# Places outside the ring for the first gate, up and input tiles, and differential heads first in the output projection

## The chip, the core and the metric

The kernel runs on one core of a Trainium2 chip. The core has a matrix engine (TensorE, PE in the profile, with its weight loads as PEld), a vector engine (VectorE, DVE), a scalar engine (ScalarE, ACT), GpSimd (POOL) and SyncE (SP). Each runs its own list of instructions in order; they wait for one another through semaphores. Data comes from HBM by DMA, which SP and POOL issue here. The metric is the device time of one execution in microseconds. Three runs of the kernel before took 2190.43 to 2191.55 us, with a median of 2191.18 us.

## The reference

Two layers of a hybrid trunk over 256 tokens of width 2048, in float32:

```python
for l in range(DEPTH):                       # 2 layers
    h = rms_norm(x, pre_mix_norm[l])
    m = hybrid_mixer(h, l, w_in[l], w_o[l], ...)
    x = x + rms_norm(m, post_mix_norm[l])
    h = rms_norm(x, pre_ffn_norm[l])
    f = swiglu(h, w_gate[l], w_up[l], w_down[l])
    x = x + rms_norm(f, post_ffn_norm[l])
```

The mixer projects h with `w_in` (2048 x 6144) into the parts of 8 stick-breaking heads and 8 differential heads, runs both kinds of attention with a norm for each head, concatenates the heads (stick-breaking ones first) and projects them with `w_o` (2048 x 2048). `swiglu` is `(silu(h @ w_gate) * (h @ w_up)) @ w_down` with an inner width of 5632.

## The kernel before

**Weights.** Almost all time goes into the products of 256 tokens with the weight matrices, and all weights pass through once. They are cut into pieces of 256 rows (a pair kp of 128-row blocks) by 512 columns (a column tile c), 512 KB each, and lie in DRAM in the order in which they are used; `weight_order` writes this order down and `plan` holds the number of each piece. A piece i goes through three steps:

- `fetch(upto)` (L201 to L228) lets SP load pieces up to number `upto`, into a ring of four "raw" buffers. A load waits until the buffer is free, that is until the lo of the piece four earlier in the ring is done.
- `feed(upto)` (L275 to L293) splits each into two parts of reduced precision, hi (a copy by ScalarE, L286) and lo = raw - hi (VectorE, L289). Both go into rings of six buffers, tags "hi" and "lo".
- `weights(i, ahead)` (L312) feeds up to `LOOKAHEAD` = 4 pieces beyond the one that is used next, and hands out the parts.

A product is then three matmuls: hi with the hi of the activations, lo with hi, and hi with lo (L536 to L538 in the output projection, L1036 to L1038 elsewhere).

**Sevens.** For some pairs kp, the gate and up pieces (or two column tiles of another matrix) are taken together as the right side of a 2 x 2 block product that needs seven products instead of eight (`seven_products`). These need sums of the two pieces. In the feed-forward part SP loads one piece into a tile G (L209) and the other into a tile T (L237), and a second DMA, issued by POOL, adds the first half of G's piece into T (L238). From G and T `mixed_weights` (L241 ff.) makes hi and lo of both, then T = T - T and G = G + T on VectorE (L267, L268), and of these Th (ScalarE, L259) and Tl (VectorE, L260). `EARLY` and `LEAD` say how far ahead of its use T is loaded. The scheduler of the framework decides in which place of SP's queue T and G come among the raws.

**Output projection.** Sixteen units first do the column tiles c = 0 and 1 (order `KP_O`), then c = 2 and 3 run over `LATE_O`, of which the pairs 5 and 6 (`O_SEVEN`) are formed as a seven. Pairs 0 to 3 are the stick-breaking heads (tiles mix_sb), 4 to 7 the differential heads (mix_df). The last two pairs, `LAST_O`, are left for an ending that is written out by hand for ScalarE and VectorE (L1131 ff.): the four units (c, kp) of token tile t = 0, each column tile then evacuated, squared and weighted (`evac_sum`, L556 to L559), `rescale` (L565 to L570 and L443 f., and L582, which adds the result to x), and then the four units of t = 1, with one group of transposes of the new x (L452, 128x128 each) behind each unit. xF, the normed and transposed x in hi and lo, comes from the transposes through ScalarE (L455) and VectorE (L460). In between stand the calls that feed and fetch the pieces that come next; their numbers are counted from `idx`, the first of the last four units: `idx` to `idx + 3` belong to the output projection, `idx + 4` and `idx + 5` are the first gate and up pieces, and so on.

**Gate and up.** Eleven column tiles of 512 follow. The first runs its pairs in the order (0, 1, 3, 2, 7, 4, 6, 5), of which 4 and 6 are sevens; its pairs 0 and 1 are done for t = 0 first and then for t = 1. The products of t = 1 begin while the transposes of t = 1 are still to come. The second column tile has sevens at 4, 5 and 6. Then come the down projection and, between the layers, the input projection of the second layer, whose activations xI come from transposes of xd (also L452), fed by `rescale` (L582).

**Rooms.** The pool `rooms` holds places of 128 x 1024 floats, four of tag "early" and four of tag "late". The early ones hold x at the start, later the mixed outputs of the differential heads, then the first four activation tiles; the late ones hold pieces and halves of x at other times. An early room of the differential heads comes free when the last unit that reads them is done.

Of the kernel before, what the change touches and what calls it, by code (L numbers as in the profile page):

```python
# [10 lines left out]
F32R = mybir.dt.float32r  # L11
# [6 lines left out]
P = 128  # L18
D = 2048
S = 256  # L20
L = 2
# [4 lines left out]
CW = 512  # L26
# [5 lines left out]
URGENT = 50  # L32
TAIL = 3
KP_O = (4, 5, 6, 7, 0, 1, 2, 3)
LATE_O = (4, 5, 0, 1, 6, 2)
LAST_O = (3, 7)
O_SEVEN = (5, 6)
PAIRS = ((6, 8), (10, 7), (9, 0), (11, 2), (1, 3), (4, 5))
IN_SEVEN = (4, 5)
# [5 lines left out]
FIRST_ORDER = (0, 1, 3, 2, 7, 4, 6, 5)  # L45
# [21 lines left out]
def weight_order():  # L67

    order = []

    def queue_pair(name, l, kp, c):
        order.append((name, l, kp, c))
        return len(order) - 1

    plan = []
    sevens, plain, own = set(), set(), set()
    for l in range(L):
        lay = {"in": {}, "o": {}, "gate": {}, "up": {}, "down": {}}
        for n, (ca, cb) in enumerate(PAIRS):
            for kp in IN_ORDER if n else range(KT // 2):  # L80
                lay["in"][ca, kp] = queue_pair("w_in", l, kp, ca)
                lay["in"][cb, kp] = queue_pair("w_in", l, kp, cb)
                if kp in IN_NOW[n]:
                    plain.add(lay["in"][cb, kp])
        order_o = [(c, kp) for kp in KP_O for c in (0, 1)]
        order_o += [(c, kp) for kp in LATE_O for c in (2, 3)] + [(c, kp) for c in (2, 3) for kp in LAST_O]
        lay["order_o"] = order_o
        for c, kp in order_o:
            lay["o"][c, kp] = queue_pair("w_o", l, kp, c)
            if c == 3 and kp in O_SEVEN:  # L90
                own.add(lay["o"][c, kp])
        for c in range(FF // CW):
            for kp in FIRST_ORDER if c == 0 else range(KT // 2):
                lay["gate"][c, kp] = queue_pair("w_gate", l, kp, c)
                lay["up"][c, kp] = queue_pair("w_up", l, kp, c)
                if kp in gate_sevens(c):
                    sevens.add(lay["up"][c, kp])
        for half in range(2):
            for kp in range(FF // P // 2):
                for c in (2 * half, 2 * half + 1):  # L100
                    lay["down"][c, kp] = queue_pair("w_down", l, kp, c)
                if kp in DOWN_SEVEN[half]:
                    sevens.add(lay["down"][2 * half + 1, kp])
        plan.append(lay)
    return order, plan, sevens, plain, own
# [48 lines left out]
def kernel(  # L154
# [18 lines left out]
    wpool = ctx.enter_context(tc.tile_pool(name="wpool", bufs=1))  # L173
# [16 lines left out]
    order, plan, sevens, plain, own = weight_order()  # L190
# [6 lines left out]
    def fetch(upto):  # L197
        while len(raws) < min(upto, len(stream)):
            i = len(raws)
            for j in range(i, min(i + EARLY + 1, mix_raw[3])):  # L200
                if j in sevens and j not in sums:  # L201
                    summed(j)
            if i in sevens:
                raws.append(sums[i])
                continue
            if i + 1 in sevens:
                g = mix_raw[0].tile([P, 2, CW], F32, tag="G", bufs=mix_raw[1], name=f"G{i}")
                with not_ahead(i):
                    loads.append(nc.sync.dma_start(g, stream[i]))  # L209
                raws.append(g)  # L210
                continue
            if i in own or i + 1 in own:
                raw = mix_pool[0].tile([P, 2, CW], F32, tag="v", bufs=2, name=f"V{i}")
            elif i in plain or i + 1 in plain:
                raw = late_room([P, 2, CW], f"GU{i}")
            else:
                raw = wpool.tile([P, 2, CW], F32, tag="raw", bufs=4, name=f"raw{i}")
            mixing = bool({i, i + 1} & (own | plain))
            with not_ahead(i) if mixing else nullcontext():
                loads.append(nc.sync.dma_start(raw, stream[i]))  # L220
            raws.append(raw)
            if not mixing:
                usual.append((i, loads[-1]))
# [3 lines left out]
    def not_ahead(i):  # L227

        return tc.issue_after(next(load.ins for j, load in reversed(usual) if j <= i - LEAD))
# [3 lines left out]
    def summed(i):  # L233

        sums[i] = mix_raw[0].tile([P, 2, CW], F32, tag="T", bufs=mix_raw[2], name=f"T{i}")
        with not_ahead(i):
            loads.append(nc.sync.dma_start(sums[i], stream[i]))  # L237
        nc.gpsimd.dma_start(sums[i][:, 0, :], stream[i - 1][:, 0, :], accum_op=ALU.add)  # L238
# [37 lines left out]
    def feed(upto):  # L276
        fetch(upto)
        while fed[0] < min(upto, len(stream)):
            i = fed[0]
            raw = raws[i]  # L280
            if i in sevens or i in plain or i in own:
                ready[i] = mixed_weights(i)
                fed[0] += 1
                continue
            hi = wpool.tile([P, 2, CW], F32R, tag="hi", bufs=6, name=f"hi{i}")
            nc.scalar.activation(hi, raw, AF.Copy)  # L286
            lo = wpool.tile([P, 2, CW], F32R, tag="lo", bufs=6, name=f"lo{i}")
            with behind():
                rest = nc.vector.tensor_tensor(out=lo, in0=raw, in1=hi.bitcast(F32), op=ALU.subtract)  # L289
            ready[i] = (hi, lo)  # L290
            fed[0] += 1
            rests.append(rest)
# [4 lines left out]
    def behind():  # L297

        if held[1] == 0:
            return nullcontext()  # L300
        held[1] -= 1
        return tc.issue_after(held[0].ins)
# [5 lines left out]
    def in_turn():  # L308

        return tc.issue_after(loads[-1].ins)  # L310

    def weights(i, ahead):  # L312
        feed(i + 1 + ahead)
        return ready[i]

    def exp_ln_tables():
# [29 lines left out]
    def late_room(shape, name, dtype=F32):  # L346

        return rooms.tile(shape, dtype, tag="late", name=name)

    def early_room(shape, name, dtype=F32):  # L350

        return rooms.tile(shape, dtype, tag="early", name=name)

    x_pool = [None]

# [237 lines left out]
    def norm_pair(pool, ob, mix, mixed, h0, gcol, nm):  # L593
# [16 lines left out]
        if nm[0] == "d":  # L610
            both = early_room([P, 2, 2, S], f"mix_{nm}", F32R)
# [403 lines left out]
    def seven_in(banks, extra, sums, xT, l, cc, kp, first, last):  # L1015
        hi, lo = weights(plan[l]["in"][cc[0], kp], LOOKAHEAD)
        m = weights(plan[l]["in"][cc[1], kp], LOOKAHEAD)
        seven_products(banks, extra, sums, *pair_blocks(xT, kp), hi, lo, m, first, last)
# [60 lines left out]
    def shared_sign(t, col):  # L1079
        return ALU.subtract if (t, col) == (1, 0) else ALU.add  # L1080

    xT = None
    for l in range(L):
# [27 lines left out]
        open_sums[0] = True  # L1111
        for kp in LATE_O:
            i, j = (plan[l]["o"][c, kp] for c in (2, 3))
            if kp not in O_SEVEN:
                for c, i in ((2, i), (3, j)):
                    unit({t: accs[c, t] for t in range(NT)}, mix, i, kp, range(NT), kp == LATE_O[0], False)
                continue
            if kp == O_SEVEN[0]:
                extra = four_banks(False, [f"{q}_o{l}" for q in ("p1", "p6", "p7", "q5")])
            hi, lo = weights(i, LOOKAHEAD)  # L1120
            m = weights(j, LOOKAHEAD)
            seven_products(got, extra, forms[kp], *pair_blocks(mix, kp), hi, lo, m, kp == O_SEVEN[0], kp == O_SEVEN[-1])
            if kp == O_SEVEN[-1]:
# [3 lines left out]
                for c in (2, 3):  # L1127
                    nc.vector.tensor_tensor(out=accs[c, 1], in0=accs[c, 1], in1=mg[1, 1][:, c - 2, :], op=shared_sign(1, c - 2))
        idx = plan[l]["o"][2, LAST_O[0]]
        last_o = [(c, kp) for c in (2, 3) for kp in LAST_O]  # L1130
        with tc.manual_schedule(engines={mybir.EngineType.Activation, mybir.EngineType.DVE}):  # L1131
            feed(idx + 6)
            for n, (c, kp) in enumerate(last_o):
                unit({0: accs[c, 0]}, mix, idx + n, kp, (0,), False, kp == LAST_O[-1], 0)
                if kp == LAST_O[-1]:
                    evac_sum(pool, accs[c, 0], mg, ssm, gpost, c, 0, f"o{l}")
            rescale(mg, ssm, 0, f"o{l}")
            for n, (c, kp) in enumerate(last_o):
                feed(idx + 7 + n)
                fetch(min(idx + 12 + n, idx + 12))  # L1140
                unit({1: accs[c, 1]}, mix, idx + n, kp, (1,), False, kp == LAST_O[-1], 0)
                transposed(0, 32 + l * KT, xT, cols=(n,))
                if (c, kp) == (2, LAST_O[-1]):
                    evac_sum(pool, accs[2, 1], mg, ssm, gpost, 2, 1, f"o{l}", True)
# [99 lines left out]
        for half in range(2):  # L1244
# [74 lines left out]
            for t in range(NT):  # L1319
# [4 lines left out]
                for c in cc:  # L1324
                    for kp in range(nkp - tail, nkp):
# [3 lines left out]
                        hi, lo = weights(plan[l]["down"][c, kp], LOOKAHEAD)  # L1329
# [66 lines left out]
```

## Time and profile before

| What | Value |
|---|---|
| median of 3 runs | 2191.18 us (2190.43 to 2191.55) |
| profiled execution | 2191.05 us |
| its span in the trace | 2189.4 us |
| granted clock of TensorE | 0.999 |
| data moved | 467.28 MB, mean 213 GB/s |
| raw loads (SP) | 522 of 512 KB, median 4.6 us from issue to landing |
| G loads (SP) | 110 of 512 KB, median 5.8 us |

A profile page gives for each engine its busy time and its number of instructions. A timeline row gives start, length, engine, line, operation, "written <- read" tiles with their shapes, how many equal instructions it joins (x4), and in brackets how long the engine had stood idle before and whose work ended that. A row of the waits view gives an engine and line, what it waited for, the sum, the number of times and the longest. A windows row gives for a stretch of time the busy time of each engine with its count of instructions, the granted clock and the DMA share. Recorded matmuls overlap, so their starts and not their lengths give the pace. Where instructions follow back to back on VectorE, the next one starts some 0.08 us before the recorded end of the last.

### The profile page before, as it was taken

What the parts mean: (1) busy time and instruction counts of PE and PEld (TensorE: products, weight loads), DVE (VectorE), ACT (ScalarE), POOL (GpSimd) and SP (SyncE); (2) the same over time, 40 slices, a digit from 0 to 9 for tenths busy, and PEclk for the clock granted to TensorE, in tenths of its full rate; (3) what the DMA queues carried; (4) which work ended last, traced back from release to release, by engine and by line L of the source; (5) the groups of instructions that cost most, each with busy time, mean ns of one, the idle gap of its engine ahead of it and who ended that gap; (6) DMA issues with size and microseconds to landing.
All of it is one profiled execution on the core that took longest, in us unless ns stands there. A gap on an engine that the chain in (4) does not pass through costs nothing.

```text
span 2189.4 us, 28540 instructions
## 1 busy us (share of the span) xinstructions
PE 2174.9 (99%) x9988; PEld 1791.1 (82%) x9988; DVE 1901.3 (87%) x2610; ACT 1370.9 (63%) x2051; POOL 139.1 (6%) x187
## 2 busy tenths in 40 slices
PE   9999999999999999999999999999999999999998
PEld 7888888888888888888878888888888888888886
DVE  6888658999999999989878886589999999999997
ACT  7666665756656656666665666657665666566664
POOL 1100000010010010000010000000000000100000
PEclk9999999999999999999999999999999999999999
DMA  9545555587687676767464555555867866767683
GB/s 327 189 164 173 192 184 172 180 281 231 219 272 229 198 258 203 247 211 260 147 241 173 177 177 185 193 168 194 277 208 255 256 210 228 238 214 233 207 266 100
DMA packets 138546, 467.28 MB, mean 213 GB/s; under 512 B 15761, under 2 KB 16785, under 8 KB 137889
## 3 DMA queue, kind: packets, MB, share of 16 engines
q1 hardware_dynamic: 122096, 436.29, 57.2%
q0 software_dynamic: 15872, 28.88, 7.5%
q8 instruction: 78, 1.28, 0.2%
q14 instruction: 68, 0.55, 0.1%
q10 hardware_dynamic: 432, 0.28, 0.0%
HBM read 457.00 MB, written 8.39 MB: 213 GB/s over the span
## 4 chain that ended last, share of the span: by engine, by line
PE 95%; DVE 3%; ACT 1%; DMA 0%; issue 0%; DVEq 0%; SPq 0%; ACTq 0%
PE c L1037 10%; PE c L1038 10%; PE c L1036 10%; PE in L1036 7%; PE in L1038 7%; PE in L1037 7%; PE dn L1280 4%; PE dn L1278 4%; PE dn L1277 4%; PE p L1037 3%; PE p L1038 2%; PE p L1036 2%; PE o L536 2%; PE o L537 2%; PE o L538 2%; PE dn L1037 1%
## 5 line engine op out<-in xcount | busy, mean ns | idle before, releaser
L289 DVE TENSOR_TENSOR lo<-raw,hi 128x1024 fp32r<-128x1024 f32 x522 | 625.4, 1219 | 97.6 <-ACT hi L286 96.6
L286 ACT ACTIVATE hi<-raw 128x1024 fp32r<-128x1024 f32 x522 | 540.6, 1055 | 186.0 <-issue 50.3
L1036 PE MATMUL c<-hi,xF 128*128 128x512 f32 x834 | 328.1, 394 | 0.1
L1037 PE MATMUL c<-lo,xF 128*128 128x512 f32 x834 | 325.1, 390 | 0.7 <-DVE lo L289 0.7
L1038 PE MATMUL c<-hi,xF 128*128 128x512 f32 x834 | 324.7, 390 | 0.0
L238 POOL DMA_DIRECT2D T<-in_weights_in_turn_dram x110 | 95.8, 871 | 1679.5 <-PE c L1037 521.3
L1037 PEld LDWEIGHTS c<-lo,xF 128*128 128x128 f32 x834 | 156.7, 188 | 33.4 <-DVE lo L289 2.5
L1038 PEld LDWEIGHTS c<-hi,xF 128*128 128x128 f32 x834 | 156.6, 188 | 32.7
L1036 PEld LDWEIGHTS c<-hi,xF 128*128 128x128 f32 x834 | 156.7, 188 | 31.4 <-ACT xF L455 0.5
L1277 PE MATMUL dn<-hi,jh 128*128 128x512 f32 x432 | 168.3, 389 | 0.0
L1278 PE MATMUL dn<-lo,jh 128*128 128x512 f32 x432 | 168.1, 389 | 0.0
L289 DVE TENSOR_TENSOR lo<-G,hi 128x1024 fp32r<-128x1024 f32 x110 | 134.1, 1219 | 29.7 <-ACT hi L286 29.7
L259 ACT ACTIVATE hi<-T 128x1024 fp32r<-128x1024 f32 x110 | 115.5, 1050 | 40.8 <-PE c L1038 26.5
L259 ACT ACTIVATE Th<-G 128x1024 fp32r<-128x1024 f32 x110 | 116.1, 1055 | 38.1 <-DVE G L268 36.2
L260 DVE TENSOR_TENSOR Tl<-G,Th 128x1024 fp32r<-128x1024 f32 x110 | 134.1, 1219 | 5.3 <-ACT Th L259 5.3
L260 DVE TENSOR_TENSOR lo<-T,hi 128x1024 fp32r<-128x1024 f32 x110 | 134.1, 1219 | 2.6 <-ACT hi L259 2.2
L268 DVE TENSOR_TENSOR G<-G,T 128x1024 f32<-128x1024 f32 x110 | 134.4, 1222 | 2.1
L259 ACT ACTIVATE Th<-T 128x512 fp32r<-128x512 f32 x110 | 68.9, 627 | 104.3 <-DVE T L267 88.3
L1280 PE MATMUL dn<-hi,jl 128*128 128x512 f32 x432 | 132.9, 390 | 0.0
L1036 PE MATMUL in<-hi,xT 128*128 128x512 f32 x328 | 131.9, 404 | 0.5 <-ACT hi L841 0.5
L1036 PE MATMUL in<-hi,xI 128*128 128x512 f32 x328 | 131.1, 401 | 0.0
L1038 PE MATMUL in<-hi,xT 128*128 128x512 f32 x328 | 128.4, 392 | 0.0
(450 smaller groups left out, 4735.6 us busy)
## 6 DMA issues: line engine op xcount, KB each, us to landing
raw<-in_weights_in_turn_dram SPq DMA_DIRECT2D x522, 512.0 KB, 4.6
T<-in_weights_in_turn_dram SPq DMA_DIRECT2D x110, 512.0 KB, 6.3
G<-in_weights_in_turn_dram SPq DMA_DIRECT2D x110, 512.0 KB, 5.8
T<-in_weights_in_turn_dram POOLq DMA_DIRECT2D x110, 256.0 KB, 7.1
GU<-in_weights_in_turn_dram SPq DMA_DIRECT2D x32, 512.0 KB, 6.2
V<-in_weights_in_turn_dram SPq DMA_DIRECT2D x8, 512.0 KB, 4.1
away_ffn<-x SPq DMA_DIRECT2D x8, 512.0 KB, 8.4
xd<-away_ffn SPq DMA_DIRECT2D x8, 512.0 KB, 8.2
```

The costliest lines, as they stand in the source:

```text
L238: nc.gpsimd.dma_start(sums[i][:, 0, :], stream[i - 1][:, 0, :], accum_op=ALU.add)
L259: nc.scalar.activation(h, w, AF.Copy)
L260: nc.vector.tensor_tensor(out=l, in0=w, in1=h.bitcast(F32), op=ALU.subtract)
L268: nc.vector.tensor_tensor(out=g, in0=g, in1=t2.unsqueeze(1).to_broadcast([P, 2, CW]), op=ALU.add)
L286: nc.scalar.activation(hi, raw, AF.Copy)
L289: rest = nc.vector.tensor_tensor(out=lo, in0=raw, in1=hi.bitcast(F32), op=ALU.subtract)
L1036: nc.tensor.matmul(a, sh, hi, start=first, stop=False, skip_group_check=open_sums[0])
L1037: nc.tensor.matmul(a, sh, lo, start=False, stop=False, skip_group_check=open_sums[0])
L1038: nc.tensor.matmul(a, sl, hi, start=False, stop=last, skip_group_check=open_sums[0])
L1277: nc.tensor.matmul(accs[c, t], sh, hi[:, kk, :], start=first, stop=False, skip_group_check=open_sums[0])
L1278: nc.tensor.matmul(accs[c, t], sh, lo[:, kk, :], start=False, stop=False, skip_group_check=open_sums[0])
L1280: nc.tensor.matmul(accs[c, t], sl, hi[:, kk, :], start=False, stop=last, skip_group_check=open_sums[0])
```

## The change

- `LATE_O` and `LAST_O` get another order: the pairs 4 to 7 (differential heads) are all done in the long part, and the pairs 2 and 3 (stick-breaking heads) are left for the ending.
- `split_tile` gives hi and lo of some pieces a place in `rooms` instead of the rings: the first gate and the first up piece of each layer (four early rooms), and of the second layer the first piece of the input projection that belongs to the seventh column tile (two late rooms). These are the pieces in `bridge`.
- `weights` does not count those pieces in its lookahead, so while they are ahead, as many others are split further ahead.
- In the ending of the output projection `feed` and `fetch` go two pieces further: `feed(idx + 8)` and `feed(idx + 9 + n)` instead of 6 and 7, and `fetch(idx + 14)` instead of `idx + 12`.

The number of instructions of each engine, their shapes and the DMAs are the same in both kernels. The order of the pieces in DRAM follows the new order of the units.

```diff
-LATE_O = (4, 5, 0, 1, 6, 2)
-LAST_O = (3, 7)
+LATE_O = (4, 5, 7, 0, 6, 1)
+LAST_O = (2, 3)
...
-            hi = wpool.tile([P, 2, CW], F32R, tag="hi", bufs=6, name=f"hi{i}")
+            hi = split_tile("hi", i)
             nc.scalar.activation(hi, raw, AF.Copy)
-            lo = wpool.tile([P, 2, CW], F32R, tag="lo", bufs=6, name=f"lo{i}")
+            lo = split_tile("lo", i)
...
+    def split_tile(tag, i):
+        if i in bridge:
+            return bridge[i]([P, 2, CW], f"{tag}{i}", F32R)
+        return wpool.tile([P, 2, CW], F32R, tag=tag, bufs=6, name=f"{tag}{i}")
+
     def weights(i, ahead):
-        feed(i + 1 + ahead)
+        upto = i + 1
+        while ahead or upto in bridge:
+            ahead -= upto not in bridge
+            upto += 1
+        feed(upto)
         return ready[i]
...
+    bridge = {}
+    for l in range(L):
+        for name in ("gate", "up"):
+            bridge[plan[l][name][0, FIRST_ORDER[0]]] = early_room
+        if l:
+            bridge[plan[l]["in"][PAIRS[0][0], 0]] = late_room
...
-            feed(idx + 6)
+            feed(idx + 8)
...
-                feed(idx + 7 + n)
-                fetch(min(idx + 12 + n, idx + 12))
+                feed(idx + 9 + n)
+                fetch(idx + 14)
```

## The prediction

> **What bounds the kernel now.** I read the page first, then the waits of TensorE, then the busy time of the stage that the change touches, then single engines inside it.
>
> ```profile
> PE 2174.9 (99%) x9988; PEld 1791.1 (82%) x9988; DVE 1901.3 (87%) x2610; ACT 1370.9 (63%) x2051; POOL 139.1 (6%) x187
> PE 95%; DVE 3%; ACT 1%; DMA 0%; issue 0%; DVEq 0%; SPq 0%; ACTq 0%
> ```
>
> TensorE is busy 99% of the span and is 95% of the chain that ended last. The change issues as many matmuls as before, so it can gain only what TensorE waits, and that is listed in full by the waits view:
>
> ```profile
> PE xT_ps L452 <- DVE xd L582: 1.3, 1, 1.3
> PE spare L367 <- DVE idle L364: 1.3, 1, 1.3
> PE p L1037 <- DVE Tl L260: 0.7, 2, 0.5
> PE c L1037 <- DVE lo L289: 0.7, 2, 0.4
> PE in L1036 <- ACT hi L841: 0.5, 1, 0.5
> PE in L1037 <- DVE lo L289: 0.3, 1, 0.3
> ```
>
> All rows together are 4.8 us. The second and the fifth belong to the start of the kernel, which the change leaves alone, so about 3.0 us are within its reach. A loss has no such ceiling, and the windows from the first gate and up matmuls to the end of the second column tile's sevens show where one would come from (columns: PE, PEld, DVE, ACT, POOL busy, clock, DMA share, GB/s):
>
> ```profile
> 394.00:418.00 24.00, 23.59 (x114) 18.74 (x113) 22.83 (x61) 22.54 (x65) 1.75 (x2) 1.00 0.65 214
> 418.00:442.00 24.00, 24.00 (x108) 19.88 (x107) 23.90 (x38) 15.57 (x18) 0.67 (x1) 1.00 0.55 194
> 442.00:454.00 12.00, 12.00 (x58) 9.96 (x57) 10.67 (x17) 7.60 (x10) 1.07 (x2) 1.00 1.04 345
> 454.00:478.00 24.00, 23.51 (x103) 18.91 (x102) 24.00 (x30) 16.35 (x19) 1.73 (x2) 1.00 0.65 195
> ```
>
> VectorE has 87% over the span, but here it is the second bound: from 418 to 478 it stands idle 0.10 + 1.33 + 0 = 1.43 us in 60. Its margin ahead of TensorE is used up at the end of that stretch, where TensorE waits for a Tl:
>
> ```profile
> 473.04 0.50 PE L1037 MATMUL p<-Tl,sh 128*128 128x512 f32 x1 [0.49 <-DVE Tl L260]
> ```
>
> So whatever delays VectorE by more than 1.4 us before 454 comes out at TensorE by 473. The same stage comes again in layer 1.
>
> **The change part by part.** All engines issue the same instructions with the same shapes; only their order and the places of some weight tiles change. Three things follow.
>
> **1. The second layer's input projection.** One weight piece more is split ahead of the transposes that wait for xd, so six 128x512 matmuls more stand before them in the built order. Matmuls start 0.227 us apart (see the q and p rows in part 3), hence 6 x 0.227 = 1.36 us of work against this wait:
>
> ```profile
> 1100.26 1.98 PE L452 MATMUL xT_ps<-ident,xd 128*128 128x128 f32 x16 [1.32 <-DVE xd L582]
> ```
>
> The price is one lo (1.22 us) more on VectorE, ahead of the evacuation that waits here anyway:
>
> ```profile
> 1083.36 0.69 DVE L556 TENSOR_TENSOR mg_d<-dn,mg_d 128x512 f32<-128x512 f32 x1 [1.60 <-PE dn L1335]
> ```
>
> 1.60 us of idle covers it. Without that cover, the evacuation chain and the transposes would be 1.22 us later, and the gain would fall to 0.1. I take -1.3 (bounds -1.4 and 0).
>
> **2. Output projection to gate and up, each layer.** The differential pairs go first, so that the rooms of their tiles are free for the hi and lo of the first gate and up pieces. VectorE and ScalarE are ordered by hand here. Before, VectorE ran three lo's and then the evacuation; now five lo's stand before it.
>
> ```profile
> 385.27 1.23 DVE L289 TENSOR_TENSOR lo<-raw,hi 128x1024 fp32r<-128x1024 f32 x1 [0.15 <-ACT hi L286]
> 386.41 0.68 DVE L556 TENSOR_TENSOR mg_o<-o,mg_o 128x512 f32<-128x512 f32 x1
> ...
> 392.02 2.74 DVE L582 SCALAR_TENSOR_TENSOR x<-mg_o,tot_o,x 128x512 f32<-128x512 f32 x4
> ```
>
> The fifth needs the second up piece. Its load still takes the ring buffer that the same lo frees, so it is issued and lands as before:
>
> ```profile
> L220 SPq DMA_DIRECT2D raw<-in_weights_in_turn_dram x1: 327/327/327, 382.8 to 382.8; - x1
> ```
>
> ```profile
> DMA to landing us min/median/max: 3.4/3.4/3.4
> ```
>
> ```profile
> 384.17 1.07 ACT L286 ACTIVATE hi<-raw 128x1024 fp32r<-128x1024 f32 x1 [0.31 <-PE o L538]
> ```
>
> It lands at 382.8 + 3.4 = 386.2, its hi ends at 387.3, its lo at 388.5. The evacuation starts there instead of at 386.41: +2.1 us, and so do the rescale (392.02 to 394.1) and the transposes (392.83 to 394.9):
>
> ```profile
> 392.36 0.39 PE L536 MATMUL o<-hi,mix_df 128*128 128x512 f32 x1
> 392.83 0.66 PE L452 MATMUL xT_ps<-ident,x 128*128 128x128 f32 x4
> ...
> 395.34 0.40 PE L538 MATMUL o<-hi,mix_df 128*128 128x512 f32 x1
> ...
> 409.54 0.60 PE L452 MATMUL xT_ps<-ident,x 128*128 128x128 f32 x4
> ```
>
> The six o rows from 392.36 to 395.34 had stood between the transposes; now they stand before them and end at 392.36 + 6 x 0.227 = 393.7. TensorE then waits 1.2 us, where it had waited 0.25 (392.36 + 0.227 to 392.83). Of this about 0.35 a layer comes back where c waited for lo (0.7 in two waits). I carry TensorE at +1.1 us at equal progress. Alone, this part would cost between -0.6 (only waits vanish) and +1.3 a layer. It decides less than the next one.
>
> **3. The T loads.** In the first column tile the sevens need T, which is loaded by SP and then added to by a DMA that POOL issues. In SP's queue the two T and two G loads stood right behind the raws of kp 7:
>
> ```profile
> 406.39 0.90 SPq L237 DMA_DIRECT2D T<-in_weights_in_turn_dram  x2
> ```
>
> ```profile
> 411.09 0.89 POOL L238 DMA_DIRECT2D T<-in_weights_in_turn_dram  x1 [260.52 <-PE c L1037]
> ```
>
> ```profile
> T<-in_weights_in_turn_dram POOLq DMA_DIRECT2D x1, 256.0 KB, 7.3
> ```
>
> T was therefore complete at 411.09 + 7.3 = 418.4. In the changed kernel three raws (both of kp 5 and the first of column tile 1) go ahead of them. The queue is in order, and the third of these raws takes the buffer that the lo of kp 7's gate frees. That lo now stands behind the xF group of token tile 1's k 8 to 11, the group at 411.60 here, whose transposes are those of 409.54:
>
> ```profile
> 410.36 1.22 DVE L289 TENSOR_TENSOR lo<-raw,hi 128x1024 fp32r<-128x1024 f32 x1
> 411.60 1.13 DVE L460 SCALAR_TENSOR_TENSOR xF<-xT_ps,gains,xF 128x128 fp32r<-128x128 f32 x4
> ...
> 420.90 1.22 DVE L260 TENSOR_TENSOR lo<-T,hi 128x1024 fp32r<-128x1024 f32 x1
> ...
> 423.17 0.68 DVE L1050 TENSOR_TENSOR sl<-s,sh 128x512 fp32r<-128x512 f32 x1
> ```
>
> Those transposes come four matmuls later in the order (59 behind the first transposes instead of 55): 409.54 + 1.1 + 4 x 0.227 - 0.35 = 411.2. Their xF group follows 2.06 later (411.60 - 409.54) at 413.3 and lasts 1.13; the lo runs from 414.5 to 415.7. The raw is issued then, which takes SP 0.33 (the L220 row above), and T at 416.1 (before, 406.39), the add 4.70 behind it (411.09 - 406.39) at 420.8, and it lands at 428.1. ScalarE's hi takes 1.06, so VectorE's lo of T starts at 429.2 instead of 420.90: +8.3 us, and VectorE stands in that wait, with everything behind it in its queue. Up to there it has split the same pieces as before; only the sl of 423.17 (0.6 back to back) and the last part of s (0.2) have moved ahead of it, which gives back 0.8. The 1.43 us of idle up to 478 give back 1.4 at best. VectorE is then 8.3 - 0.8 - 1.4 = 6.1 us late at 473, where it had no margin, and TensorE with it: **+6.1 us a layer**, which holds part 2 as well, since TensorE's own 1.1 us lie inside it.
>
> The bounds. From below: if VectorE finds slack that the windows do not show, TensorE waits for the chain of the first T alone. Its first matmul with T's hi was
>
> ```profile
> 427.70 0.39 PE L1036 MATMUL q<-hi,sh 128*128 128x512 f32 x1
> ```
>
> and the lo of T now ends at 429.2 + 1.2 = 430.4: 2.7 us, less the 0.49 of the row at 473.04, hence +2.2 a layer. From above: the loads may take their usual time instead of that of this place,
>
> ```profile
> T<-in_weights_in_turn_dram SPq DMA_DIRECT2D x110, 512.0 KB, 6.3
> ```
>
> ```profile
> T<-in_weights_in_turn_dram POOLq DMA_DIRECT2D x110, 256.0 KB, 7.1
> ```
>
> 6.3 + 7.1 against 4.70 + 7.3 is 1.4 more, and the idle may not come back: 8.3 - 0.8 + 1.4 = +8.9 a layer. I take 6.1, since the windows speak for a full VectorE.
>
> [...]
>
> The sum: 2191.05 (the profiled execution; its span is 2189.4 and 1.65 lie around it) + 2 x 6.1 - 1.3 = 2202.0. The median of the runs, 2191.18, is 0.13 above the profiled one, which I neglect. As both uncertain give-backs pull down rather than up, I put the forecast at **2201 us**.
>
> **The rivals.**
>
> **A, not slower:** the T's are not missed. The mechanism is the lookahead: raws, hi and lo of four further pieces are ready and TensorE works on kp 5 and column tile 1 while T is late. For it speaks that the built order does pull some matmuls of those forward; against it, that they are about ten, or 2.3 us, and that VectorE's idle time is lost whatever TensorE does. Then the waits go instead: 3.0 us off, 2188 us. It decides if T lands before about 421.
>
> **B, a small loss:** VectorE recovers most of its delay in the second column tile, and only the lower bound stays: 2191.05 + 2 x 2.2 - 1.3 = 2194. For it speaks that 442 to 454 has slack; against it the 24.00 of 24 behind it.
>
> [...]
>
> **How the numbers follow.** About 0.2%, 4.4 us, is what a measurement of this kernel can tell from no change: faster is below 2186.8, slower above 2195.6. The forecast has 0.58, A 0.16, B 0.18, C 0.08. A reaches below 2186.8 in half of its cases; of B one in five lies above 2195.6, and of the forecast nearly all. That gives faster 0.08, same 0.08 + 0.14 + 0.01 = 0.23 and slower 0.69. The range runs from just under B's time to the upper bound short of C together with slow loads (2191.05 + 2 x 8.9 - 1.3 = 2207.6): 2192 to 2207. The forecast's own range is 2197 to 2207.
>
> **What would show it.** Part 1: the 1.32 us before the transposes of xd gone. Part 2: the first xT_ps of layer 0 near 394.9. Part 3: SP issuing the first T near 416 instead of 406.39, POOL's add near 421, a VectorE wait of several us for ScalarE's hi of T, and new TensorE waits of the p, q and c groups for that hi and lo, 3 us or more in all by 442 and again in layer 1. I am wrong if the T's are issued before 411, or if VectorE shows the wait and TensorE does not.

## The result, and the profile after

| | median | runs |
|---|---|---|
| before, measured with it | 2191.02 us | 6, 2190.26 to 2191.55 |
| changed kernel | 2203.11 us | 6, 2202.16 to 2204.43 |

The ratio is 1.0054, with a 95% interval of 1.0043 to 1.0065: slower by 12.1 us, where 2201 (2192 to 2207) was forecast. The profiled execution after has a span of 2201.4 us, 12.0 more than the 2189.4 before.

The page after, its busy times and its chain:

```profile
PE 2180.0 (99%) x9988; PEld 1790.3 (81%) x9988; DVE 1902.1 (86%) x2610; ACT 1370.8 (62%) x2051; POOL 139.5 (6%) x187
PE 92%; DVE 4%; DMA 2%; ACT 1%; issue 1%; SPq 0%; DVEq 0%; ACTq 0%; POOLq 0%
```

The counts are those of before. The busy time of TensorE grew by 5.1 us only; in the chain TensorE has 92% (95% before), VectorE 4% (3% before) and DMA 2% (0% before). Where TensorE waits is told by the waits view (engine and line, what it waited for, sum, times, longest):

```profile
PE xT_ps L469 <- DVE x L599: 2.3, 2, 1.2
PE q L1053 <- ACT hi L259: 1.8, 2, 1.5
PE q L1054 <- DVE lo L260: 1.5, 2, 0.8
PE c L1053 <- ACT hi L286: 1.5, 2, 1.2
PE spare L384 <- DVE idle L381: 1.3, 1, 1.3
PE p L1054 <- DVE Tl L260: 0.8, 3, 0.3
...
PE p L1054 <- DVE lo L289: 0.8, 1, 0.8
PE p L1053 <- ACT Th L259: 0.6, 2, 0.5
```

The wait of xT_ps for xd is gone. One of 1.1 to 1.2 us in each layer before the first transposes of x is new, and so is a family of waits in the first sevens: for hi and lo of G and T, for Th, for Tl. How many matmuls stand in equal stretches shows their size, the windows of 418 to 442 and of 1512 to 1536, before

```profile
418.00:442.00 24.00, 24.00 (x108) 19.88 (x107) 23.90 (x38) 15.57 (x18) 0.67 (x1) 1.00 0.55 194
1512.00:1536.00 24.00, 24.00 (x108) 19.87 (x107) 23.89 (x33) 14.96 (x17) 1.72 (x2) 1.00 0.56 190
```

and after:

```profile
418.00:442.00 24.00, 20.05 (x80) 13.95 (x78) 16.65 (x27) 12.78 (x15) 1.75 (x2) 1.00 0.45 139
1512.00:1536.00 24.00, 21.30 (x76) 15.39 (x75) 15.55 (x26) 11.93 (x15) 1.75 (x2) 0.86 0.42 123
```

28 matmuls fewer at 0.227 us are 6.4 us in layer 0; 32 fewer are 7.3 in layer 1. VectorE is busy 7.3 us less in the same 24 us of layer 0: it waits too. In layer 1 the granted clock is 0.86 over the stretch, of which more below.

To set times of the two traces side by side one offset is needed. The same VectorE instructions just before the ending begin at 380.35 before,

```profile
380.35 1.29 DVE L1128 TENSOR_TENSOR o<-o,mg_o 128x512 f32<-128x512 f32 x2
```

and 1.63 us earlier after:

```profile
378.72 1.28 DVE L1145 TENSOR_TENSOR o<-o,mg_o 128x512 f32<-128x512 f32 x2
```

The 1.63 come from the first ten microseconds, which the change does not touch: the first ten matmuls of the input projection start between 6.25 and 10.23 us before, the last of them 0.43 us apart, and between 6.40 and 8.52 after, the last of them some 0.23 apart. Below, "moved by" has the 1.63 added. The timeline after, PE, SP, POOL and VectorE of the stage:

```profile
393.33 1.32 PE L469 MATMUL xT_ps<-ident,x 128*128 128x128 f32 x8 [1.11 <-DVE x L599]
```

```profile
402.95 11.89 SPq L220 DMA_DIRECT2D raw<-in_weights_in_turn_dram  x3
414.89 0.90 SPq L237 DMA_DIRECT2D T<-in_weights_in_turn_dram  x2
415.83 0.91 SPq L209 DMA_DIRECT2D G<-in_weights_in_turn_dram  x2
```

```profile
419.57 0.89 POOL L238 DMA_DIRECT2D T<-in_weights_in_turn_dram  x1 [270.64 <-DVE s L1063]
```

```profile
413.26 1.22 DVE L289 TENSOR_TENSOR lo<-raw,hi 128x1024 fp32r<-128x1024 f32 x1
425.38 1.23 DVE L289 TENSOR_TENSOR lo<-G,hi 128x1024 fp32r<-128x1024 f32 x1 [4.80 <-ACT hi L286]
428.38 1.23 DVE L260 TENSOR_TENSOR lo<-T,hi 128x1024 fp32r<-128x1024 f32 x1 [1.78 <-ACT hi L259]
```

The last of the three raws ahead of the T loads is issued at 414.5, when the lo that began at 413.26 has ended. The first transposes moved by 2.1 us, the first T load by 10.1 (406.39 to 414.89 + 1.63), POOL's add by 10.1, and VectorE's lo of the first T by 9.1. The chain of waits from 414 to 436 has this link in it, the longest of all its pieces:

```profile
419.57 7.65 DMA T<-in_weights_in_turn_dram
```

What TensorE lost is read where both kernels have the same order again, at the first transposes of the activations: before

```profile
449.46 0.60 PE L1229 MATMUL actT_ps<-ident,w 128*128 128x128 f32 x4
```

and after

```profile
454.76 0.60 PE L1246 MATMUL actT_ps<-ident,w 128*128 128x128 f32 x4
```

5.30 + 1.63 = 6.9 us in layer 0. The waits that the timeline shows for TensorE up to there are eight and sum to 5.1 us; each costs some 0.27 more than its row says, because it is counted from the recorded end of a matmul, 0.39 after its start where the next would start after 0.227, and because the matmul behind it holds up the next for 0.33 (the one of 426.66 after, with the next at 426.99). That makes 7.3, an estimate. The loss is 6.6 at the next column tile (492.82 to 497.77) and stays so. Between the layers 1.3 us are gained, and layer 1 then loses 8.2 (1538.23 to 1550.07 at the same place is 11.84, less 4.95 - 1.3 that it brought along). Together, 6.6 - 1.3 + 8.2 - 1.63 = 11.9, which is the difference of the two spans.

### The profile page after: what moved, and what is told of

It reads as the page before. It is cut to its first block, busy times and chain, and to the rows that moved or that the text cites. A ratio compares the mean times of both kernels' runs of the same rounds, so it can differ in the third digit from the quotient of the medians.

```text
span 2201.4 us, 28546 instructions
## 1 busy us (share of the span) xinstructions
PE 2180.0 (99%) x9988; PEld 1790.3 (81%) x9988; DVE 1902.1 (86%) x2610; ACT 1370.8 (62%) x2051; POOL 139.5 (6%) x187
## 4 chain that ended last, share of the span: by engine, by line
PE 92%; DVE 4%; DMA 2%; ACT 1%; issue 1%; SPq 0%; DVEq 0%; ACTq 0%; POOLq 0%
PE c L1055 9%; PE c L1053 9%; PE c L1054 9%; PE in L1053 7%; PE in L1055 7%; PE in L1054 7%; PE dn L1297 4%; PE dn L1295 4%; PE dn L1294 4%; PE p L1054 2%; PE p L1053 2%; PE p L1055 2%; PE o L555 2%; PE o L553 2%; PE o L554 2%; DVE lo L289 1%
## 5 line engine op out<-in xcount | busy, mean ns | idle before, releaser
L1053 PE MATMUL in<-hi,xT 128*128 128x512 f32 x328 | 131.0, 401 | 0.8 <-DVE xT L831 0.8
L1054 PE MATMUL in<-lo,xI 128*128 128x512 f32 x328 | 128.0, 390 | 0.3 <-DVE lo L289 0.3
```

Source lines behind the costliest of these rows:

```text
L1053: nc.tensor.matmul(a, sh, hi, start=first, stop=False, skip_group_check=open_sums[0])
L1054: nc.tensor.matmul(a, sh, lo, start=False, stop=False, skip_group_check=open_sums[0])
```

## The experiments

Two theories stood at the start. Theory Q: the place of the T loads in SP's queue costs the time. Theory E: the two lo's ahead of the evacuation cost it, since VectorE is full there. Each batch had the kernel before on the same chip, with medians of 2191.69 (runs 1 to 4), 2191.60 (5 to 8) and 2190.64 us (9 and 10).

**Run 1, T and G loads first.** In `fetch`, the loads of the four pieces behind the first sevens are ordered behind the G load:

```diff
...
+    for lay in plan:
+        last = lay["gate"][0, FIRST_SEVEN[-1]]
+        for j in range(2, 6):
+            behind_g[last + j] = last
...
-            with not_ahead(i) if mixing else nullcontext():
+            with not_ahead(i) if mixing else tc.issue_after(g_loads[behind_g[i]].ins) if i in behind_g else nullcontext():
                 loads.append(nc.sync.dma_start(raw, stream[i]))
```

> The changed kernel with one thing moved: the raw loads of kp 5 and of the first pair of column tile 1 are queued behind the T and G loads of the first sevens. Theory Q (the place of the T loads in SP's queue costs the time): T is issued well before 407 again, the waits of the p, q and c groups between 424 and 442 vanish, and the time falls by about 2 x 7 to 2189 us (2187 to 2191), since the input gain of 1.3 stays. Theory E (the two lo's put ahead of the evacuation cost it, because VectorE is full in this stage): the late T only shows that delay, and the time stays above 2199 us.

Measured: 2191.83 us (10 runs), ratio to before 1.0001 (0.9991 to 1.0010). The T loads are issued at

```profile
399.66 0.90 SPq L244 DMA_DIRECT2D T<-in_weights_in_turn_dram  x2
```

and of the 12.1 us over the kernel before 0.1 is left with one change in SP's order (by the medians of the two batches, 2203.11 - 2191.83, 11.3 are gone). Theory Q holds. The 2189 were not reached, though, and 2191.83 lies above the range: the longest wait of this run behind the start of the kernel,

```profile
PE xT_ps L476 <- DVE x L606: 1.8, 2, 1.0
```

is one that the kernel before did not have. That is the second part of the prediction by itself.

**Run 2, only the blocking raw behind them.** The same with `range(4, 6)`.

> A smaller dose: the two raws of kp 5 stay ahead of the T loads, only the raw of column tile 1 that waits for the lo of kp 7's gate goes behind them. Theory Q: that one raw holds the queue, so T is issued near 406 as in the kernel before and the time is that of the run with all raws behind, 2189 us (2187 to 2192). If the number of raws ahead counts, and not the wait of the last of them, two thirds of the loss remain, about 2199 us. Theory E: above 2199 us.

Measured: 2192.09 us (10 runs), ratio 1.0003 (0.9994 to 1.0012).

```profile
407.13 0.90 SPq L244 DMA_DIRECT2D T<-in_weights_in_turn_dram  x2
```

T is issued 7.5 us later than in run 1, and the time is the same within the intervals, 0.1 above the range. It is the one raw that waits for the lo of kp 7's gate, and not the number of raws ahead; and T at 407 is early enough.

**Run 3, the input places alone.** The kernel before with `split_tile`, the new `weights`, and in `bridge` only the piece of "in".

> The kernel before with the late places for the first input tile of layer 1 alone. By the prediction's first part the wait of 1.32 us before the transposes of xd goes and nothing else moves: 2189.7 us, 1.3 below the kernel before. Rival: VectorE's additional lo pushes the evacuation and nothing is gained, 2191.0 us.

Measured: 2189.97 us (10 runs), ratio 0.9992 (0.9983 to 1.0001), 1.7 us below before. In its trace the sixteen transposes of xd start without a wait (1.32 before):

```profile
1099.54 1.98 PE L467 MATMUL xT_ps<-ident,xd 128*128 128x128 f32 x16
```

**Run 4, three lo's ahead of the evacuation.**

```diff
-            feed(idx + 8)
+            feed(idx + 6)
```

> The changed kernel with the first call of the ending set back to feed(idx + 6), so that three lo's and not five stand ahead of the evacuation. Theory Q: the raw of column tile 1 still stands ahead of the T loads, which come perhaps 1 us earlier; the time falls by 2 us at most, to 2201 to 2203 us. Theory E: nearly all of the loss goes, 2189 to 2192 us.

Measured: 2202.76 us (4 runs), ratio 1.0051 (1.0035 to 1.0068). Theory E falls: the evacuation is early again, and the loss stays. T is as late as in the changed kernel, not 1 us earlier, and the lo's taken away in front now stand between the rescale and xF:

```profile
414.92 0.92 SPq L237 DMA_DIRECT2D T<-in_weights_in_turn_dram  x2
```

```profile
396.87 0.50 PE L1055 MATMUL c<-hi,xF 128*128 128x512 f32 x1 [1.37 <-DVE xF L477]
```

Runs 5 to 7 have T and G first, as in run 1, and ask what is left of the ending.

**Run 5, feed(idx + 7) as the first call.**

> The kernel with all raws behind the T and G loads (2191.8 us), and the first call of the ending at feed(idx + 7): four lo's instead of five ahead of the evacuation. Theory P (what is left of the loss is the wait for the first transposes, because the evacuation starts two lo's later): the transposes come about 1.1 us earlier in each layer, and nearly all of it reaches the end, 2189.6 to 2190.2 us. If the stage is bound by VectorE's total work, the place of one lo moves nothing, 2191.8 us.

Measured: 2190.34 us (11 runs), ratio 0.9993 (0.9985 to 1.0002), 0.1 above the range of theory P.

**Run 6, feed(idx + 6).**

> The same with feed(idx + 6): three lo's ahead of the evacuation. The transposes come as early as in the kernel before (a wait of 0.25 us instead of 1.1 to 1.3), but the two lo's now stand between the rescale and the first xF group on VectorE, where the run with feed(idx + 6) alone showed TensorE waiting 1.5 us for xF in each layer. Theory P: one wait for another, 2191.3 to 2192.3 us. If the late evacuation costs by itself, 2189.5 us.

Measured: 2192.02 us (11 runs), ratio 1.0001 (0.9992 to 1.0010). Its waits show the exchange: none for x before the transposes is left, and the one for xF is there in both layers, as in run 4:

```profile
PE c L1062 <- DVE xF L484: 2.8, 2, 1.4
```

**Run 7, the lo's spread thinly.**

```diff
-            feed(idx + 8)
+            feed(idx + 7)
...
-                feed(idx + 9 + n)
+                feed(idx + (8, 9, 10, 11)[n])
```

> T and G loads first, feed(idx + 7), and after it one piece for each of the four units (idx + 8 to idx + 11), so that the lo's are spread as thinly as in the kernel before. Theory P: as with feed(idx + 7), and less in front of xF: 2189 us (2188 to 2190), below the kernel before and below the input places alone. If VectorE's total binds, 2191.8 us.

Measured: 2189.47 us (11 runs), ratio 0.9991 (0.9982 to 1.0000), 2.1 below before. Theory P holds in all three: the time follows the wait before the transposes or before xF, with VectorE's total unchanged. The differences are small against the intervals, but in this batch every execution of run 7, and all but one of run 5, lie below every one of run 6. This is the lowest time of a kernel that does the whole work; run 3, with 2189.97, cannot be told apart from it.

**Run 8, the order of the pairs alone.** The kernel before with the new `LATE_O` and `LAST_O`.

> The kernel before with the new order of the pairs in the output projection alone. All theories: the same work in the same places, 2191.7 us; if the late differential heads had been gating the units, it would be faster.

Measured: 2191.28 us (11 runs), ratio 0.9999 (0.9990 to 1.0008). No difference.

**Runs 9 and 10, less for VectorE behind the late T.** In `feed`, of the changed kernel (9) and of the kernel before (10):

```diff
+    no_lo = {lay[name][0, FIRST_ORDER[-1]] for lay in plan for name in ("gate", "up")}
...
             nc.scalar.activation(hi, raw, AF.Copy)
+            if i in no_lo:
+                ready[i] = (hi, hi)
+                fed[0] += 1
+                continue
```

> The changed kernel without the two lo's of kp 5 in the first column tile of each layer (the products use hi in their place), that is 2.3 us less on VectorE right behind the late T, with SP's queue unchanged. Theory F (the late T costs through VectorE, which is full and hands its lateness on): TensorE loses some 2 us less in each layer, 2198 to 2199 us. Theory C (TensorE waits link by link for the chain T, hi, lo, Th, Tl, whatever else VectorE has to do): at most the last links come earlier, 2201.5 to 2203 us.

> The kernel before without the same lo's, as the base for that run. Theory F: the two waits for Tl at the end of the second column tile go, 0.5 us a layer, 2190.5 us, so that the distance of the two kernels shrinks from 12 to about 8. Theory C: 2190.5 to 2191.5 us, and the distance stays above 11.

Measured: run 9 2202.19 us (4 runs, 2200.04 to 2205.74), ratio 1.0052 (1.0037 to 1.0067); run 10 2189.31 us (10 runs), ratio 0.9992 (0.9982 to 1.0001). The distance of the medians is 12.9 us, above the 11 of theory C (link by link, not the rival C of the prediction). Run 10 itself lies below what either theory had for it: without these lo's the kernel before gains 1.3 us. The trace of run 9 is that of its fastest execution, 2200.04 us, with a granted clock of 0.999; the other three had 0.996 or 0.997 and took 2201.81 to 2205.74, so the median holds time at a lower clock. Without it the distance is 10.7, between the two theories and nearer to C. The waits of run 9 from 418 to 445 are again those for the chain itself:

```profile
PE c L1058 <- ACT hi L287: 1.2, 1, 1.2
PE q L1058 <- ACT hi L260: 1.0, 1, 1.0
PE q L1059 <- DVE lo L261: 0.8, 1, 0.8
PE p L1059 <- DVE lo L294: 0.3, 1, 0.3
```

The wait for Th is gone from this list and so is that for Tl, and the first transposes of the activations come earlier: at that place run 9 is 5.0 us behind run 10 in layer 0 (453.51 against 449.14, and 0.60 for the offset of their starts, found as above), where the changed kernel is 6.9 behind the kernel before. That is the 2 us of theory F. But the scheduler also put the second column tile in another order here, with a wait for a Tl at its end (0.8 us at 476, the same in layer 1), and at the next ending, in layer 1, the loss is back at 6.0, with the 1.3 gained between the layers added again, against 6.7. So the two runs do not decide between the theories: over the whole layer the distance hardly changes, with the order of the second column tile changed as well, and in the first column tile VectorE's load may have up to 2 us of the loss.

## Why the prediction was right, and where not

**Part 1, the input projection: -1.3.** Right in mechanism and size: run 3 measured -1.7 (the interval allows -3.7 to +0.2), and its trace and the one after have the transposes of xd without a wait.

**Part 2, the ending: +1.1 carried, +1.3 as its upper bound alone.** Right. The evacuation starts two lo's later, the transposes moved by 2.1 us as worked out, and TensorE waits 1.11 us where 1.2 had been put. That it costs by itself is shown by run 1 against run 3, 2191.83 - 2189.97 = 1.9, or 0.9 a layer, and by run 7, which takes it away. (The two also differ in the order of the pairs, which changed nothing in run 8, and in the T loads, which come earlier in run 1.) The prediction counted it as lying inside part 3. By subtraction the runs have 0.9 for it and 11.3 / 2 = 5.6 for the T loads, with what they cost in granted clock, on top: 6.5 a layer where 6.1 was the forecast. Whether the two add up or lie inside one another these runs do not separate.

**Part 3, the T loads.** The place was right, and the steps hold to within a microsecond, all moved by about 10 us:

| step | forecast | in the trace, + 1.63 |
|---|---|---|
| T issued | 416.1 | 416.5 |
| POOL's add issued | 420.8 | 421.2 |
| T complete | 428.1 | 428.9 (419.57 + 7.65) |
| VectorE's lo of T | 429.2 | 430.0 |
| TensorE late, layer 0 | 6.1 | 6.6 |

Runs 1 and 2 show that this is the cause: some 11 us of the loss hang on one raw in SP's queue.

The step that failed is how the late T reaches TensorE. The prediction had VectorE full, without slack, handing 6.1 us on by 473; the direct chain was only the lower bound, 2.2. In the trace VectorE stands idle for 4.80 and 1.78 us ahead of the late G and T, TensorE waits at once, between 425 and 441, link by link (3.8 us in the rows; 3.0 in layer 1), and behind 449 nothing is lost any more. The bound was too low because it ended at the lo of the first T. Behind that stand a hi of a raw that ScalarE's order puts behind those of T (1.2 us of wait), Th (0.5) and Tl (0.3); and in front of it the G's, which were loaded right after T and came as late: lo of G is the first wait of all, 0.8. VectorE's load is not out of it, though. From the lo of T on it is busy without a gap up to 445, and the last of these links stand in its queue among other work, while TensorE from 449 to 478 has no gap (columns as above):

```profile
428.38:445.00 16.62, 13.86 (x53) 9.59 (x54) 16.61 (x22) 11.06 (x13) 0.00 (x0) 1.00 0.28 100
449.00:478.00 29.00, 29.00 (x132) 23.46 (x130) 28.18 (x41) 18.76 (x23) 2.60 (x3) 1.00 0.80 260
```

How much of the loss is the bare chain and how much VectorE's full queue behind T stays open; run 9 leaves up to 2 us a layer to the latter. That the number came out near is partly luck: the loss arose in another place and by other waits than forecast, and was of about the same size.

**The rivals.** A (not slower) fell with the pulled-forward matmuls: they do not cover the wait, and the kernel is 12 us slower. B (VectorE recovers) fell too: the loss at the end of the second tile is 6.6 against 6.9 at its start. C, a larger loss, has its 0.08 by the author's estimate alone, and the range ends "short of C" by it: no run shows where it would begin. What the runs showed of a larger loss is in layer 1, where the granted clock falls to 0.50 just behind waits of 1.50 and 0.76 us, the window

```profile
1524.40:1531.00 6.60, 6.17 (x14) 4.02 (x13) 6.35 (x11) 5.05 (x7) 0.00 (x0) 0.50 0.00 1
```

and the matmuls in it start 0.43 us apart, not 0.227:

```profile
1524.45 0.63 PE L1054 MATMUL c<-lo,sh 128*128 128x512 f32 x1
1524.88 0.63 PE L1055 MATMUL c<-hi,sl 128*128 128x512 f32 x1
```

Eleven to twelve such steps at +0.2 are some 2.3 us, an estimate. That is more than the difference of the layers (8.2 against 6.9), since the waits in layer 1 sum to 3.0 us and those in layer 0 to 3.8. In layer 0 of this execution the clock did not fall (1.00 in the windows from 418 to 445). The forecast of 2201 lies 2 us under the median, about the size of this.

## What to carry to other kernels

When a scheduler orders a DMA queue, compare that order and what each entry waits for: one load that waits for a buffer holds up the loads behind it, whoever needs them (here T from 407.13 us in run 2 to 414.89), and neither the instruction counts nor the diff show it. Take the room from an added lookahead only as far as the work that is due next is not pushed back by it: here five splits ahead of the evacuation cost 0.9 us a layer and four, with the rest spread, nothing that could be measured. When bounding a wait, follow the chain to its last link on every engine that takes part, not to the first use of the late data.

## What the runs showed of the hardware that was not expected

The granted clock drops to 0.50 behind waits of which the longest is 1.50 us. In layer 1 after, TensorE stood for 1.50 us (q for hi of T) and then for 0.76 with one matmul between; 1520 to 1524 hold 7 matmuls only, and 1524.40 to 1531 run at a clock of 0.50. In run 4 the same is seen in layer 0, after waits of 1.19, 0.76, 1.17 and 0.45 us:

```profile
434.60:437.80 3.20, 3.20 (x9) 2.43 (x9) 2.83 (x5) 1.76 (x3) 0.00 (x0) 0.50 0.00 0
```

The longest wait does not decide it: in layer 1 of run 4 the waits were 1.57, 0.76, 1.16 and 0.45 us, and the clock stayed at 1.00. The clock of 0.50 lasts 6.83 us after and some 3.4 in run 4. The 3.4 us just ahead of the drop after, those ahead of the drop in run 4, and a stretch of the same length among the waits in run 4's layer 1, which kept the clock, are:

```profile
1520.91:1524.33 3.42, 1.24 (x4) 0.83 (x5) 2.02 (x3) 3.11 (x4) 0.00 (x0) 1.00 0.08 13
431.19:434.60 3.41, 1.78 (x7) 1.21 (x7) 3.41 (x7) 3.41 (x5) 0.00 (x0) 1.00 0.00 0
1520.04:1523.46 3.42, 1.85 (x8) 1.00 (x6) 0.47 (x1) 1.56 (x2) 0.00 (x0) 1.00 0.74 135
```

TensorE was busy for 1.24 and 1.78 us of them ahead of the two drops, and for 1.85 where the clock stayed. What decides whether it drops, these three stretches do not show.
